# An encoder block on eight cores: a build-time list scheduler for all engines, paired score matmuls, and weights cast through SBUF

## The chip, the cores and the metric

The kernel runs on all eight cores of one Trainium2 chip (two dies of four cores). Each core computes two of the sixteen sequences; the cores exchange nothing. The metric is the device time of the slowest core in microseconds (us), the median of several executions. Such a program has a second, slower state in some of its executions, in which the cores of one die or of both show a lower granted TensorE clock. TensorE is written PE, VectorE DVE, ScalarE ACT, GpSimd POOL; PEld is PE's weight load, which overlaps its matmuls. PV is the matmul of the exponentiated scores with v. Filler is work without a wait of its own (mostly FFN matmuls) that PE runs while an attention step waits. A slab is a block of weights, and a ring is the set of SBUF buffers through which slabs pass.

## The reference, cut to what matters

```python
# x: (16, 2048, 1024) float32; 2 sequences a core
h = rms_norm(x, norm1_g)
lru_x, lru_gate, q, k, v = split(h @ w_in)        # 1024 -> 2560, five slabs of 512 columns
# head group A: causal conv (width 4), RG-LRU (exp, log, scan over positions), times GeLU(lru_gate)
out_a = gelu(lru_gate) * rg_lru(causal_dwconv(lru_x))
# head group B: differential attention, 4 heads, two softmax maps a head (c = 0, 1) over 64 channels each
logits = q_c k_c^T / 8 + bias[rel_bucket(k_pos - q_pos)]          # block-causal in chunks of 64
out_b = rms_norm((softmax_1 - lam * softmax_2) @ v, per head)
x = x + concat(out_a, out_b) @ w_out
# gated FFN, width 3072, causal conv (width 3) on the gate branch
h = rms_norm(x, norm2_g)
gate, val = split(h @ ffn_w_up)                   # 1024 -> 2 x 3072
x = x + (gelu(causal_dwconv(gate)) * val) @ ffn_w_down
out = rms_norm(x, final_norm_g)
```

A core works through eight groups of 512 tokens (four to a sequence). Group g of a sequence attends to the keys of groups 0 to g, so attention grows from group to group and starts small again with the second sequence. The FFN of a group depends only on that group's own mix, apart from two columns of conv history. So the FFN of group g-1 (only matmuls, conv and GELU) can run beside the attention and LRU of group g (short steps with long waits).

## The kernel before

It is written straight through, and an instruction's place on its engine is the place of its call. A helper derives the semaphore waits from the buffers read and written:

```python
def op(self, eng, fn, reads=(), writes=()):
    waits = self._deps(eng, reads, writes)
    self.ecount[eng] += 1
    tok = (("e", eng), self.ecount[eng])
    self.prog[eng].append((fn, waits, tok[0], 1))      # order of calls = order of execution
    self._update(reads, writes, tok)
```

The overlap is made by hand: a window takes the list of attention and LRU steps of group g and the list of FFN units of group g-1, and puts a number of FFN units after each step by a table of weights.

```python
def weight(n):                              # how many FFN units a step deserves
    kind, h, key, _ = users[n]
    if kind == "lru":
        return 1.5
    if kind == "norm":
        return 3.0
    ...
for cur in range(nU):                       # run_window (cut)
    issue(cur + dpt, cur - 1)               # scores one step ahead
    ...
    target = int(math.ceil(cumw[cur + 1] / cumw[nfu] * nF - 1e-9))
    batch = fu[fi:target]                   # FFN units placed here
    ...
    users[cur][1](slot(cur))                # exp and PV of this step
```

Attention handles one softmax map c at a time. Score tiles rotate over two PSUM banks. A tile near the diagonal gets its bias on DVE into SBUF and then a second exp:

```python
op("pe", lambda e: e.matmul(banks[bk][:, 0:N], lhsT=KT[c * 64:(c + 1) * 64, h, j * 128:(j + 1) * 128],
                            rhs=qT[c * 64:(c + 1) * 64, h, q0:G], start=True, stop=True), ...)
if wn:
    op("dve", lambda e: e.tensor_tensor(out=sbn[:, p, 0:wn], in0=banks[bk][:, 0:wn], in1=bias_ap, op=ALU.add), ...)
...
if wn:
    op("act", lambda e: e.activation(out=PT[:, p, 0:wn], in_=sbn[:, p3, 0:wn], func=AF.Exp), ...)
if N > wn:
    op("act", lambda e: e.activation(out=PT[:, p, wn:N], in_=banks[bk][:, wn:N], func=AF.Exp, bias=...), ...)
```

The FFN beside attention owns three PSUM banks, and the down projection of four token tiles therefore goes in passes of at most three accumulators, reading its weights twice:

```python
na = len(acc_banks)                         # 3 beside attention
passes = [list(range(NT))[i:i + na] for i in range(0, NT, na)]
for c2 in range(2):
    for ts in passes:
        accs = acc_banks[:len(ts)]
        for ks in range(3):
            units.append((lambda ...: unit_down(c2, ks, ts, accs), nop, False))
```

The weights arrive as float32 and are needed as bf16. Twenty-five copies, issued by POOL, cast them from HBM to HBM at the start. Every use then loads a slab of 1 MB into a ring of three.

```python
def cast_slab(si, parts):
    for pi, (c0, ncol, src) in enumerate(parts):
        S_.dma("pool", wsl_d[si, :, :, c0:c0 + ncol], src.rearrange("(kk p) c -> p kk c", p=128), ...)
def load_slab(si):
    r = ring_i[0]
    ring_i[0] = (r + 1) % NRING
    S_.dma("sp", ring[:, r, :, :], wsl_d[si], reads=b_slabd[si], writes=[b_ring[r]])
```

The softmax here doesn't subtract the row's maximum and nothing guards it: scores larger than these inputs give would overflow.

## Time and profile before

| | before |
|---|---|
| time, median of 3 fast runs | 2580.04 us (2579.63 to 2582.57) |
| profiled core's span | 2570.9 us |
| PE busy | 1996.0 us, 78% |
| DVE, ACT busy | 1240.6, 1144.8 us (48%, 45%) |
| mean granted clock, eight cores | 0.875 to 0.885 |
| bytes moved | 317.49 MB |

Read such a profile from the engine that does the unavoidable work. Here that is PE. A PE busy for 78% at a mean clock of 0.88 loses twice: in the idle time, and in matmuls that run slowly after it. Next comes the question of what ended the idle time (the waits view), and where in the span it lies (a cut into stretches). The lines themselves stand in the prediction below.

### The profile page before, as it was taken

How to read it: one execution, taken by the hardware profiler on the slowest of the kernel's cores; microseconds unless marked ns; L12 is line 12 of the kernel's file. 1: busy time of each engine (PE TensorE's matmuls, PEld its weight loads, DVE VectorE, ACT ScalarE, POOL GpSimd, SP SyncE). 2: the span in 40 equal slices, each digit the busy share in tenths (PEclk: the TensorE clock that was granted, in tenths of full speed). 3: DMA queues.
4: the chain of work that ended last, by engine and by line, in shares of the span. 5: the costliest groups of instructions: out<-in, count | busy, mean ns of one | idle time of the engine just before them, and what ended most of it. 6: DMA issues, size and time to landing. Idle time of an engine off the chain costs nothing.

```text
span 2570.9 us, 32883 instructions; the slowest of 8 cores (2560.0 to 2570.9 us)
## 1 busy us (share of the span) xinstructions
PE 1996.0 (78%) x9920; PEld 892.2 (35%) x9920; DVE 1240.6 (48%) x2666; ACT 1144.8 (45%) x1861; POOL 143.3 (6%) x152
## 2 busy tenths in 40 slices
PE   1637879688896887979787598878779687788787
PEld 1213334333343333434333343334334343333333
DVE  1355562554625535244663465355563454533562
ACT  1244552545535454454442454344553455545240
POOL 1000000000000000000000000000000000000000
PEclk8758999698996978978999699979899798998899
DMA  9999935431244311343225332443214421124233
GB/s 186 174 108 152 177 105 189 152 107 74 82 164 148 115 49 67 112 185 113 99 99 197 117 129 84 163 180 108 73 68 178 164 99 66 65 91 154 104 129 115
DMA packets 70523, 317.49 MB, mean 123 GB/s; under 512 B 5328, under 2 KB 30928, under 8 KB 39248
## 3 DMA queue, kind: packets, MB, share of 16 engines
q1 hardware_dynamic: 44352, 289.18, 31.9%
q0 software_dynamic: 26000, 26.22, 9.7%
q8 instruction: 85, 1.39, 0.2%
q14 instruction: 86, 0.70, 0.1%
HBM read 324.81 MB, written 42.99 MB: 143 GB/s over the span
## 4 chain that ended last, share of the span: by engine, by line
PE 57%; DVE 16%; ACT 11%; issue 8%; DMA 4%; another core or an unknown queue 2%; POOL 1%; DVEq 1%; ACTq 0%; SPq 0%; POOLq 0%
PE pb L497 26%; PE pb L892 13%; PE pb L818 5%; PE pb L707 5%; PE pb L672 5%; ACT PT L698 3%; DVE aT L511 2%; DVE facc L516 2%; PE pb L592 2%; ACT aT L868 2%; DMA ring<-wslab 2%; DMA wslab<-w_in 2%; ACT facc L506 2%; DVE facc L523 1%
## 5 line engine op out<-in xcount | busy, mean ns | idle before, releaser
L497 PE MATMUL pb<-hT,ring 128*128 128x512 bf16 x4096 | 1003.1, 398 | 80.3 <-DMA ring<-wslab 30.0
L497 PEld LDWEIGHTS pb<-hT,ring 128*128 128x128 bf16 x4096 | 392.0, 101 | 596.9 <-issue 215.1
L707 PE MATMUL pb<-Va,PT 128*128 128x129 bf16 x2176 | 257.0, 243 | 301.4 <-ACT PT L698 254.8
L698 ACT ACTIVATE PT<-pb,prm 128x512 bf16<-128x512 f32 (+3 forms) x512 | 302.1, 608 | 229.4 <-PE pb L672 206.8
L892 PE MATMUL pb<-ring,aT 128*128 128x512 bf16 x1536 | 348.4, 382 | 12.2 <-DMA ring<-wslab 5.5
L707 PEld LDWEIGHTS pb<-Va,PT 128*128 128x128 bf16 x2176 | 161.2, 105 | 471.1 <-issue 424.5
L506 ACT ACTIVATE facc<-pb,prm 128x512 f32<-128x512 f32 x192 | 149.1, 776 | 258.1 <-PE pb L497 175.7
L672 PE MATMUL pb<-qT,KT 64*128 64x512 bf16 (+3 forms) x640 | 237.3, 400 | 8.0 <-ACT thi L645 5.1
L685 DVE TENSOR_TENSOR sbn<-pb,prm 128x256 f32<-128x256 f32 (+1 forms) x304 | 110.3, 371 | 274.7 <-PE pb L672 225.3
L694 ACT ACTIVATE PT<-sbn 128x256 bf16<-128x256 f32 (+1 forms) x304 | 112.0, 372 | 293.6 <-DVE sbn L685 272.2
L884 DVE TENSOR_TENSOR aT<-pb,aT 128x512 bf16<-128x512 f32 x192 | 129.5, 689 | 219.4 <-PE pb L497 195.9
L516 DVE SCALAR_TENSOR_TENSOR facc<-pb,prm,facc 128x511 f32<-128x511 f32 x192 | 143.7, 748 | 149.6 <-ACT facc L506 142.8
L892 PEld LDWEIGHTS pb<-ring,aT 128*128 128x128 bf16 x1536 | 145.0, 98 | 189.8 <-issue 26.8
L511 DVE SCALAR_TENSOR_TENSOR aT<-pb,prm,facc 128x510 bf16<-128x510 f32 x192 | 143.7, 748 | 20.0
L818 PE MATMUL pb<-ring,mixT 128*128 128x512 bf16 x512 | 129.8, 421 | 8.0 <-ACT mixT L801 6.5
L516 DVE SCALAR_TENSOR_TENSOR xc<-pb,prm,xc 128x511 f32<-128x511 f32 (+2 forms) x96 | 71.7, 748 | 112.7 <-ACT xc L506 105.8
L902 DVE TENSOR_TENSOR xg<-pb,xg 128x512 f32<-128x512 f32 x64 | 42.8, 687 | 130.3 <-PE pb L892 116.2
L472 PE MATMUL pb<-ident,hb 128*128 128x128 bf16 x512 | 46.6, 270 | 74.5 <-ACT hb L460 36.0
L433 POOL TENSOR_TENSOR sm<-sm 128x4 f32<-128x4 f32 x36 | 36.3, 1008 | 1186.3 <-DVE sm L424 1186.3
L672 PEld LDWEIGHTS pb<-qT,KT 64*128 64x128 bf16 x640 | 57.1, 95 | 128.1 <-issue 94.7
L868 ACT ACTIVATE aT<-aT 128x2048 bf16<-128x2048 bf16 x48 | 88.2, 1899 | 0.2
L523 DVE SCALAR_TENSOR_TENSOR facc<-fhalo,prm,facc 128x1 f32<-128x1 f32 (+1 forms) x288 | 67.7, 235 | 31.9 <-DVE facc L523 1.6
(105 smaller groups left out, 1468.7 us busy)
## 6 DMA issues: line engine op xcount, KB each, us to landing
ring<-wslab SPq DMA_DIRECT2D x242, 1024.0 KB, 4.9
xg<-x SPq DMA_DIRECT2D x32, 512.0 KB, 6.9
out<-xg SPq DMA_DIRECT2D x32, 512.0 KB, 2.8
wslab<-w_up POOLq DMA_DIRECT2D x12, 1024.0 KB, 88.6
wslab<-w_down POOLq DMA_DIRECT2D x6, 1024.0 KB, 108.2
wslab<-w_in POOLq DMA_DIRECT2D x5, 1024.0 KB, 56.6
wslab<-w_out POOLq DMA_DIRECT2D x2, 1024.0 KB, 99.7
prm<-params SPq DMA_DIRECT2D x1, 1098.5 KB, 7.2
```

The source lines that it names most:

```text
L497: last = e.matmul(banks[bi][:], lhsT=ring[:, r, kk, c * 128:(c + 1) * 128], rhs=src[:, kk, :], start=(kk == 0), stop=(kk == 7))
L506: op("act", lambda e: e.activation(out=acc, in_=ps[:], func=AF.Identity, scale=w_ap[:, nh:nh + 1], bias=b_ap), reads=[b_ps[bi], b_prm], wr ...
L511: op("dve", lambda e, sft=sft, j=j: e.scalar_tensor_tensor(out=last_out[:, sft:G], in0=ps[:, 0:G - sft], scalar=w_ap[:, j:j + 1], in1=acc[ ...
L516: op("dve", lambda e, sft=sft, j=j: e.scalar_tensor_tensor(out=acc[:, sft:G], in0=ps[:, 0:G - sft], scalar=w_ap[:, j:j + 1], in1=acc[:, sf ...
L672: op("pe", lambda e: e.matmul(banks[bk][:, 0:N], lhsT=KT[c * 64:(c + 1) * 64, h, j * 128:(j + 1) * 128], rhs=qT[c * 64:(c + 1) * 64, h, q0 ...
L694: op("act", lambda e: e.activation(out=PT[:, p, 0:wn], in_=sbn[:, p3, 0:wn], func=AF.Exp), reads=[b_sbn[p3]], writes=[b_PT[p]])
L698: op("act", lambda e: e.activation(out=PT[:, p, wn:N], in_=banks[bk][:, wn:N], func=AF.Exp, bias=prm[:, fo + h:fo + h + 1]), reads=[b_ps[b ...
L707: last = e.matmul(banks[abk][:, off:off + 129], lhsT=PT[:, p, (il - i0) * 128:(il - i0 + 1) * 128], rhs=Va[:, j, h, 0:129], start=(j == 0 ...
L818: last = e.matmul(banks[bk][:], lhsT=mixT[:, kk, t * 128:(t + 1) * 128], rhs=ring[:, r, kk, :], start=(kk == 0), stop=(kk == 7))
L868: op("act", lambda e, k4=k4: e.activation(out=aT[:, 4 * k4:4 * k4 + 4, :], in_=aT[:, 4 * k4:4 * k4 + 4, :], func=AF.Gelu_apprx_tanh), read ...
L884: op("dve", lambda e: e.tensor_tensor(out=aT[:, fc, :], in0=banks[bV][:], in1=aT[:, fc, :], op=ALU.mult), reads=[b_ps[bV], b_aT[fc]], writ ...
L892: last = e.matmul(banks[bk][:], lhsT=aT[:, ks * 8 + kk, t * 128:(t + 1) * 128], rhs=ring[:, r, kk, :], start=(ks == 0 and kk == 0), stop=( ...
```

## The change

Its intent is to leave the order to a program. Every call now makes a node with an estimated duration, its reads and writes, a priority and the engines that may run it. A list scheduler simulates the engines at build time, always places the node that can start first (on a tie the one of higher priority), gives out PSUM banks and ring slots as it goes, and only then emits the instructions. Attention steps of group g+1 have higher priority than the FFN of group g, which fills what is left. At the same time: the two maps of a score are computed by two matmuls on different halves of the array into two neighbouring banks, with one bias add in PSUM and one exp over both; the 25 slabs become 50 halves of 0.5 MB, loaded as float32 on first use, cast by ACT or DVE and written back for later uses; conv history moves to POOL in one go.

```diff
+    def schedule(self, policy):
+        ...
+        while placed < len(nodes):
+            best = None
+            for e in engs:
+                for n in avail[e]:                       # (condensed)
+                    t = n.ready + slack.get(e, 0.0)
+                    if t < free[e]: t = free[e]
+                    for v in n.opens:                    # PSUM bank or ring slot that this node opens
+                        f = find_slots(v, t, used)
+                        ...                              # no slot: node can't be placed now
+                    if e == "act" and n.tab is not None and n.tab != cur_tab:
+                        tt = t + (6.0 if left.get(cur_visit, 0) else 1.4)
+                    key = (tt, n.pri, n.i)
+        ...
+        for n, t in order:
+            self._emit_node(n)
...
-NRING = 3
+    NRA, NRF, NPT = 4, 5, 4          # ring halves of projections, of the FFN; exp tiles
...
-        def cast_slab(si, parts): ...                    # HBM to HBM
+            if key not in seen:
+                node({"sp": 0.1}, ... dma_start(out=stg_ap[g.s], in_=src), writes=[g], dma=1048576, tag="ldw")
+                node({"dve": ..., "act": ...}, cast, reads=[g, b_stg], writes=[v, fifo], tag="cast")
+                node({"sp": 0.1}, ... dma_start(out=wsl_d[si], in_=ring[:, v.s, :]), reads=[v], tag="wb")
+            else:
+                node({"sp": 0.1}, ... dma_start(out=ring[:, v.s, :], in_=wsl_d[si]), dma=524288, tag="ld")
...
+                    s = VT(P_ps, n=2, cls="qk")          # two neighbouring banks, always 0 and 1
+                    def qk(e, s=s, j=j, N=N, h=h, i0=i0):
+                        for c in range(2):
+                            last = e.matmul(psum[:, s.s + c, 0:N], lhsT=KT[c * 64:(c + 1) * 64, ...],
+                                            rhs=qT[c * 64:(c + 1) * 64, h, i0 * 128:G], start=True, stop=True)
...
+                    op("act", act_us(2 * N, ptr=1), ... e.activation(out=PT[:, pt.s, :, 0:N],
+                        in_=psum[:, s.s:s.s + 2, 0:N], func=AF.Exp, bias=pv("farb", h, h + 1)), ...)
...
+                accs = [VT(P_ps) for t in range(NT)]     # down projection: four accumulators at once
+                for ks in range(3):
+                    sl = [load_slab(("dn", c2 * 3 + ks, hf), P_F, ringF, pr) for hf in range(2)]
+                    for hf, t in [(hf, t) for hf in range(2) for t in range(NT)]:
+                        op("pe", MMC / 2, f, reads=[sl[hf][0]] + b_aT[...], writes=[accs[t]], tag="dn")
...
+        for gi in range(ngrp):
+            mix, ffn = (gi + 1) * 1000, (gi + 1) * 1000 + 500
+            stage_at(stage_A, mix, gi + 1)               # norm, q, k, v
+            units, convs = stage_at(stage_F1, ffn, gi)
+            stage_at(stage_G, ffn + 1, gi + 1, [units[21]], gi)
+            stage_at(stage_F2, ffn + 2, gi, convs, gi)
+            stage_at(stage_L, mix + 8, gi + 1)           # LRU
+            stage_at(stage_B, mix + 10, gi + 1)          # attention
+            stage_at(stage_C, mix + 20, gi + 1)          # output projection, norm 2
+            stage_at(stage_E, ffn + 5, gi)
+        def slots(v, p):
+            if v.cls == "qk": return (0,)
+            if v.cls == "acc": return (2, 3, 4)          # PV accumulators
+            if attn[1] == 0 and attn[2] == 0:            # no attention step open
+                return (5, 6, 7, 4, 3, 2, 1, 0)
+            return (5, 6, 7)
```

(In the diff many lines are cut, and the loop of the scheduler is condensed.)

## The prediction

> **What bounds the kernel now.** I read the cores view first (eight spans from 2560.0 to 2570.9 us, dies equal, no core at a capped clock), then the page. Its busy list and its slices in tenths say that no engine is full:
>
> ```profile
> PE 1996.0 (78%) x9920; PEld 892.2 (35%) x9920; DVE 1240.6 (48%) x2666; ACT 1144.8 (45%) x1861; POOL 143.3 (6%) x152
> ...
> PEclk8758999698996978978999699979899798998899
> DMA  9999935431244311343225332443214421124233
> ```
>
> PE is busy 78% and the clock dips: 575 us of the span hold no matmul, and part of the 1996 runs slow. DMA is full only in the first five slices (325 us). To see where the idle lies I cut the span at the V projections (end of a group's input stage) and at the first output-projection matmul, which gives "overlap windows" (attention and LRU of group g with the FFN of g-1) and "transitions" (output projection, norms, input projection). Columns: stretch, length, busy of PE, PEld, DVE, ACT, POOL with counts, clock, DMA share, GB/s.
>
> ```profile
> 0.00:109.00 109.00, 46.41 (x192) 20.48 (x192) 20.92 (x47) 21.15 (x34) 12.52 (x21) 0.83 0.99 178
> 109.00:202.00 93.00, 28.91 (x137) 11.89 (x136) 53.41 (x108) 45.17 (x101) 7.52 (x9) 0.52 1.05 125
> ...
> 863.00:1157.50 294.50, 235.72 (x1194) 103.13 (x1193) 128.02 (x285) 148.28 (x241) 16.39 (x16) 0.85 0.28 102
> 1157.50:1221.00 63.50, 58.03 (x290) 28.02 (x290) 27.88 (x52) 25.89 (x41) 0.61 (x1) 0.90 0.31 111
> 1221.00:1441.00 220.00, 156.57 (x712) 66.25 (x711) 123.83 (x277) 84.34 (x137) 17.33 (x16) 0.88 0.39 139
> ```
>
> Group 0 takes 202 us with 75 us of matmul, at half clock in its second part. In the later windows DVE and ACT are busy 38 to 56%, PE 71 to 80%, at clock 0.85 to 0.88. So the bound is latency in a hand-made order: PE meets a step whose input is not there yet and holds up FFN matmuls that could run. The waits view names it:
>
> ```profile
> PE pb L707 <- ACT PT L698: 254.8, 170, 12.8
> PE pb L794 <- DVE ob L743: 61.3, 8, 10.3
> PE pb L707 <- ACT PT L694: 44.1, 34, 4.1
> PE pb L472 <- ACT hb L460: 36.0, 2, 29.2
> ```
>
> (us in total, times, longest.) The PV matmuls wait 299 us for exp, and the transposes wait 61 us at each group's end for the head norm.
>
> **What the Trainium skill says.**
> - "TensorE: Matmul & The Clock Gate", Part 1, The HAM clock gate: PE idle for a window of about 3.4 us falls to half clock and returns when busy. The trace agrees: 0.52 in 109 to 202 us, 1.00 in 1040 to 1105 us where PE is busy 95%. Filling gaps therefore pays twice.
> - The same Part 1 also warns of a limit of 13/16 of the clock once three cores of a die run dense matmuls. The trace differs: from 2515 to 2540 us all eight cores run 115 to 118 matmuls in 25 us (about 0.215 us each), and every one shows 1.00.
> - The same page, Part 3, row tiling: matmuls with a short contraction on different row groups run at once. The timeline agrees: two score matmuls together take what one takes.
>
> ```profile
> 1042.58 0.39 PE L672 MATMUL pb<-qT,KT 64*128 64x512 bf16 x2
> ...
> 1050.37 0.39 PE L672 MATMUL pb<-qT,KT 64*128 64x512 bf16 x1
> ```
>
> - "DMA: Bandwidth & Descriptors", Specifications: about 358 GB/s from HBM per core. The trace: 289.18 MB of the hardware queue in 31.9% of 2570.9 us are 353 GB/s while active.
>
> **The change part by part.**
> 1. *PE work.* The instruction orders of the two programs have the same matmuls (6464 of 512 columns, 640 scores, 2176 PV, 640 transposes). In issue slots at full clock: 6464 x 0.216 (the timeline has 8 in 1.73 us) = 1396; PV 2176 x 0.08 (4 in 0.32) = 174; transposes 640 x 0.09 (46.6 us / 512) = 58. Score slots: before, only 50 of the 320 pairs stand side by side, so 590 slots; after, all 320 do. At about 0.3 us a slot (0.32 for 512 columns, less for short ones) 177 becomes 96. The floor is 1805 us before and 1724 after. Pairing itself saves 81 us of PE.
> 2. *exp and tables.* Rows for 512, 384, 256 and 128 columns (683, 580, 473, 367 ns) give 262 + 0.82 per column, so one exp over 1024 costs 1.10 us. After: 224 x 1.10 + 32 x (0.89 + 0.68 + 0.47) = 312 us, against 302.1 + 112.0 before. One LRU activation less per block saves 32 x 0.63 = 20. Table loads fall from 49 x 1.283 us to about 20, saving 37. Added are 37 weight casts of about 1.9 us (the row of 2048 columns, L868), 70 us. ACT goes from 1145 to about 1056 us. DVE stays near 1230: halo steps -68, casts and LRU steps about +60. Neither was the bound; over 1890 us they are 56% and 65%.
> 3. *Order.* FFN steps are now halves of 4 matmuls (0.86 us), placed between score and PV by estimated times, over any group boundary; the FFN of g starts while the norms of g are still running, so the transitions lose their idle ends. By group: 808 x 0.216 + 80 x 0.09 = 181.7 us without attention (124.4 of it FFN), plus attention of 11.2, 26.2, 41.3, 56.3 us for g = 0 to 3 of a sequence (PV x 0.08 plus pairs x 0.3).
> 4. *Weights.* The 25 casting copies through HBM, issued one per 8 to 16 us until 217 us, go. Instead 50 halves of 1 MB come into two staging buffers, are cast by ACT or DVE, and are written back. For group 0, 14 halves at about 5.5 us (estimate: 1.05 MB at 250 GB/s is 4.2, plus cast and waits) after 13 us of x and parameters make 90 us; attention overlaps, the last projection ends near 115 instead of 218 us. The 36 FFN halves fall into the first overlap window: 36 x 1.57 MB (read and write-back) + about 10 MB of other loads = 67 MB, which at 285 GB/s (below the 353, for 1 to 2 KB rows) is 235 us against 208 us of PE work. That window is DMA-bound.
> 5. *Sum.* 115 (group 0) + 235 + six windows of PE work, 6 x 181.7 + 41.3 + 56.3 + 11.2 + 26.2 + 41.3 + 56.3 = 1323, times 1.06 for stalls that the order cannot foresee (a choice: dense stretches now run at 1.00 to 1.03 of the floor, mixed ones far worse) = 1402 + last FFN and final norm 139 = 1891 us; about 1895 as timed.
>
> **The rivals.**
> - *Imperfect order.* An engine executes the fixed order; where real latencies differ from the estimate, PE waits for exp as now. Scores have one pair of PSUM banks, so a step of score, bias, exp is a serial chain of about 0.32 + 0.1 + 1.1 + 0.3 = 1.8 us; 64 of them are 117 us within a 238 us window. For it: the 299 us of such waits now. Against: a score then has an FFN half to fill its wait. At 1.15 instead of 1.06 the time is 2010.
> - *First use bound by DMA.* If 1 KB rows give only 170 GB/s, the first window takes 390 us instead of 235 and the time is 2050. For it: the casting copies hold the DMA at 0.97 to 1.06 for 325 us today. Against: those move DRAM to DRAM with a cast.
> - *Clock cap.* If unbroken matmuls on all cores trip the 13/16 limit, 1724/0.8125 = 2122 replaces 1724: about 2300. Against: the eight cores at 1.00 above.
> - *PSUM bound.* With attention alive, only three banks serve projections; a gate unit holds one for about 1.73 + 0.78 + 2 x 0.75 + waits = 4.6 us, so one unit per 1.5 us, just under PE's 1.73. It holds, narrowly; a 20% longer hold costs perhaps 60 us.
>
> **Range and chances.** All rivals but the cap leave a gain above 20%, and even the cap leaves 10%. Better than predicted means stalls of 1.02 and a first window at the PE floor: about 1805. Worse means one of the first two rivals in full: about 2030. To come within 2%, several rivals must meet; I give that 3%, slower 1%, faster 96%.
>
> **What would show it.** In the changed profile: PE busy about 90% or more in the middle slices, clock 0.97 to 1.00; the waits of PV for exp below 100 us; 320 score pairs in half the slots; exp over 1024 near 1.10 us; DMA high only until about 350 us; group 0's output projection over by about 115 us; ACT near 1056, DVE near 1230. It would be wrong if the clock reads 0.81 on a die, if the middle windows stay under 85% PE, or if the first window runs past 300 us.

## The result, and the profile after

The changed kernel takes **2089.38 us** (median of four fast runs, 2082.57 to 2095.6) against 2580.14 us for the kernel before in the same rounds. The ratio is 0.809, 95% interval 0.8055 to 0.8121. Ratios in this document are the mean time of one kernel's fast runs over that of the other's of the same rounds, so not quite the ratio of the medians quoted. The direction was right. The time lies outside the range of about 1805 to 2030: the gain is 491 us where 685 were expected.

The same parts of the page as before, busy time and slices in tenths, of the changed kernel:

```profile
PE 1804.5 (86%) x9920; PEld 845.4 (40%) x9920; DVE 1087.7 (52%) x2137; ACT 1070.6 (51%) x1350; POOL 170.1 (8%) x251
...
PEclk9859899999999999879989998999999999977999
DMA  9874478953224623026324541345331462302534
```

PE's busy time fell by 191.5 us and its idle time from 574.9 to 289.6 us. A slice is 52 us long. After the start the clock column is lowest at two places, 840 to 940 us (8, 7) and 1830 to 1940 us (7, 7). DMA is high until about 420 us, with a lull (4) from 157 to 262 us.

To hold the result against the prediction's sum I cut the span at the last down-projection matmul of each group (the first cut is the end of group 0's output projection). Columns: stretch, length, busy of PE, PEld, DVE, ACT, POOL with counts, clock, DMA share, GB/s.

```profile
0.00:167.00 167.00, 85.47 (x440) 39.86 (x440) 79.23 (x150) 98.36 (x128) 20.91 (x36) 0.80 0.79 231
167.00:424.80 257.80, 217.68 (x1145) 98.78 (x1144) 140.00 (x270) 143.56 (x157) 16.95 (x26) 0.94 0.70 218
...
679.40:961.70 282.30, 252.19 (x1481) 122.80 (x1480) 134.64 (x263) 152.53 (x190) 20.54 (x28) 0.90 0.32 109
961.70:1183.40 221.70, 198.68 (x1001) 91.73 (x1000) 128.20 (x258) 100.07 (x143) 19.81 (x30) 0.95 0.39 134
...
1670.80:1951.50 280.70, 250.63 (x1481) 121.90 (x1480) 134.39 (x263) 152.41 (x190) 20.44 (x27) 0.91 0.30 103
1951.50:2094.00 142.50, 126.35 (x576) 54.94 (x574) 69.71 (x144) 37.41 (x45) 6.22 (x8) 0.97 0.43 149
```

| term of the sum | predicted, us | measured, us | difference |
|---|---|---|---|
| group 0 to its output projection | 115 | 167 | +52 |
| first window | 235 | 258 | +23 |
| six windows | 1323 x 1.06 = 1402 | 1526.7 = 1323 x 1.154 | +125 |
| last FFN and final norm | 139 | 142.5 | +3 |

The windows are the stretches between two cuts; the floor is the prediction's sum of PE's issue slots at full clock. The largest miss is the factor on the six windows. Their PE is idle for 151.5 us, and its busy time is 52 us above the floor. I read these 52 us as the lowered clock (0.90 to 0.96 in these windows); with experiment 1's clock of 0.96 to 0.99 the same windows have 1332 us of busy PE, 9 above the floor.

The groups that concern attention (columns: line, engine, operation, shapes, count, busy time and mean ns of one, then idle time before them and what ended most of it):

```profile
L959 ACT ACTIVATE PT<-pb,prm 128x1024 bf16<-128x1024 f32 (+1 forms) x320 | 314.9, 984 | 248.4 <-PE pb L941 96.6
...
L941 PE MATMUL pb<-qT,KT 64*128 64x512 bf16 (+3 forms) x640 | 125.6, 384 | 97.9 <-ACT PT L959 97.4
L968 PE MATMUL pb<-Va,PT 128*128 128x129 bf16 x2176 | 201.2, 239 | 4.7 <-ACT PT L959 3.0
```

PV (L968) waits 3.0 us for exp where it waited 299 before. The wait has partly moved to the next score (L941), which waits 97.4 us until exp has emptied the one pair of score banks. That is a third of the old wait. The timeline of PE shows a part of it in a long attention, where PE has no FFN matmul left to put in between (start, duration; x is the number of matmuls in a run; brackets hold the idle time before and its releaser):

```profile
862.81 0.39 PE L941 MATMUL pb<-qT,KT 64*128 64x512 bf16 x2
863.13 0.63 PE L968 MATMUL pb<-Va,PT 128*128 128x129 bf16 x8
863.60 1.03 PE L1099 MATMUL pb<-ringF,aT 128*128 128x512 bf16 x4
...
866.42 0.39 PE L941 MATMUL pb<-qT,KT 64*128 64x512 bf16 x2 [0.85 <-ACT PT L959]
866.74 0.63 PE L968 MATMUL pb<-Va,PT 128*128 128x129 bf16 x8
868.22 0.39 PE L941 MATMUL pb<-qT,KT 64*128 64x512 bf16 x2 [0.85 <-ACT PT L959]
...
915.20 9.63 PE L1099 MATMUL pb<-ringF,aT 128*128 128x512 bf16 x36
```

Until 864.6 us every score and PV is followed by four matmuls of the down projection (L1099). Then they are gone for 50 us. At 915.2 us, when the last PV of the attention is done, they come back in one run of 36. A step now takes 1.8 us (866.42 to 868.22): this is the serial chain of score, exp and PV that the prediction's first rival had described, and the filler that was to hide it is missing. The same stretch in columns as above, and two others that matter later:

```profile
840.00:865.00 25.00, 25.00 (x173) 11.95 (x172) 8.83 (x16) 12.47 (x13) 1.02 (x1) 1.00 0.11 38
865.00:915.00 50.00, 31.74 (x220) 18.86 (x220) 11.70 (x21) 23.80 (x25) 1.01 (x1) 0.56 0.00 1
125.00:150.00 25.00, 2.61 (x8) 0.69 (x8) 14.21 (x26) 15.18 (x22) 7.33 (x10) 0.50 0.81 225
1040.00:1050.00 10.00, 4.85 (x29) 2.76 (x30) 9.55 (x22) 6.49 (x11) 0.61 (x1) 0.58 0.00 0
```

With filler PE is busy 25.00 of 25 us at clock 1.00. Without it 31.7 of 50 at 0.56. These 31.7 us hold some 22 steps; at the 0.95 us that score and PV take at 866.42 us, they would be 21 us (an estimate). In the third line PE has next to nothing to do at the end of group 0. In the fourth DVE is busy for 9.55 of 10 us.

**Why the filler ends: a lock-out** (read from the code and the trace). While attention runs, the scheduler gives other work three banks, 5, 6 and 7. The down projection opens four accumulators of one bank each. Three can be opened, and the fourth tile of each weight half has to wait for a bank until attention is over. The weight halves that this tile still needs stay in the FFN ring, and the ring has five. So three tiles x five halves x four matmuls = 60 matmuls can run, and the trace has 60 of them between 841.5 and 864.6 us. After that nothing of the FFN can go on. This lies in the two groups with the longest attention (the windows of 282 and 281 us); the second one has its 60 matmuls between 1831 and 1854 us and then the same 50 us without filler.

### The profile page after: what moved, and what is told of

The parts are those of the page before. It is cut to its first block, busy times and chain, and to the rows that moved or that the text cites. A ratio compares the mean times of both kernels' runs of the same rounds, so it can differ in the third digit from the quotient of the medians.

```text
span 2094.1 us, 30805 instructions; the slowest of 8 cores (2073.4 to 2094.1 us)
## 1 busy us (share of the span) xinstructions
PE 1804.5 (86%) x9920; PEld 845.4 (40%) x9920; DVE 1087.7 (52%) x2137; ACT 1070.6 (51%) x1350; POOL 170.1 (8%) x251
## 4 chain that ended last, share of the span: by engine, by line
PE 60%; ACT 11%; issue 10%; DMA 9%; DVE 8%; POOL 1%; SPq 0%; DVEq 0%; ACTq 0%; POOLq 0%
PE pb L774 28%; PE pb L1099 13%; PE pb L792 7%; PE pb L968 5%; PE pb L941 4%; ACT PT L959 4%; DMA ringA<-wslab 3%; ACT facc L1058 2%; DMA ringF<-wslab 2%; DMA Va<-w_down 2%; PE pb L745 1%; DVE aT L1064 1%; ACT aT L1078 1%; DMA KT<-w_in 1%; DMA Va<-w_up 1%
## 5 line engine op out<-in xcount | busy, mean ns | idle before, releaser
L774 PE MATMUL pb<-hT,ringF 128*128 128x512 bf16 x3072 | 734.6, 389 | 44.5 <-DVE aT L1069 12.5
L774 PEld LDWEIGHTS pb<-hT,ringF 128*128 128x128 bf16 x3072 | 290.2, 100 | 409.9 <-issue 115.7
L959 ACT ACTIVATE PT<-pb,prm 128x1024 bf16<-128x1024 f32 (+1 forms) x320 | 314.9, 984 | 248.4 <-PE pb L941 96.6
L1099 PE MATMUL pb<-ringF,aT 128*128 128x512 bf16 x1536 | 355.3, 386 | 13.1 <-ACT ringF L705 10.7
L774 PE MATMUL pb<-hT,ringA 128*128 128x512 bf16 x1024 | 242.8, 387 | 24.2 <-ACT ringA L705 6.2
L1099 PEld LDWEIGHTS pb<-ringF,aT 128*128 128x128 bf16 x1536 | 147.8, 99 | 194.6 <-issue 37.9
L941 PE MATMUL pb<-qT,KT 64*128 64x512 bf16 (+3 forms) x640 | 125.6, 384 | 97.9 <-ACT PT L959 97.4
L968 PE MATMUL pb<-Va,PT 128*128 128x129 bf16 x2176 | 201.2, 239 | 4.7 <-ACT PT L959 3.0
L968 PEld LDWEIGHTS pb<-Va,PT 128*128 128x128 bf16 x2176 | 153.6, 106 | 86.2 <-issue 53.8
L758 POOL TENSOR_TENSOR sm<-sm 128x1 f32<-128x1 f32 (+1 forms) x128 | 94.2, 743 | 1140.5 <-DVE sm L755 1053.9
L774 PEld LDWEIGHTS pb<-hT,ringA 128*128 128x128 bf16 x1024 | 98.0, 99 | 146.3 <-issue 43.8
L792 PE MATMUL pb<-ringA,mixT 128*128 128x512 bf16 x512 | 116.5, 383 | 11.2 <-POOL mixT L913 11.2
L941 PEld LDWEIGHTS pb<-qT,KT 64*128 64x128 bf16 x640 | 35.2, 94 | 179.6 <-issue 167.2
```

The lines of the kernel that those rows point to most:

```text
L758: op("pool", 1.0, lambda e: e.tensor_tensor(out=smv(rsn, 0, n), in0=smv(ssn, 0, n), in1=smv("mhalf").to_broadcast([128, n]), op=ALU.pow), ...
L774: last = e.matmul(bank(p), lhsT=w[:, kk, cc * 128:(cc + 1) * 128], rhs=src[:, kk, :], start=(kk == 0), stop=(kk == 7))
L792: last = e.matmul(bank(p), lhsT=src[:, hf * 4 + kk, t * 128:(t + 1) * 128], rhs=w[:, kk, :], start=(hf == 0 and kk == 0), stop=(hf == 1 an ...
L941: last = e.matmul(psum[:, s.s + c, 0:N], lhsT=KT[c * 64:(c + 1) * 64, j // NT, h, (j % NT) * 128:(j % NT + 1) * 128], rhs=qT[c * 64:(c + 1 ...
L959: op("act", act_us(2 * N, ptr=1), lambda e, s=s, pt=pt, N=N, h=h: e.activation(out=PT[:, pt.s, :, 0:N], in_=psum[:, s.s:s.s + 2, 0:N], fun ...
L968: last = e.matmul(psum[:, acc[ab].s, off:off + 129], lhsT=PT[:, pt.s, c, (il - i0) * 128:(il - i0 + 1) * 128], rhs=Va[:, j, h, 0:129], sta ...
```

## The experiments

The windows are numbered 1 (ending at 424.8 us in the changed kernel) to 8. Every edit is against the changed kernel. The list scheduler plans the whole program anew after each edit, so an edit moves more than it names; differences below about 20 us are hard to put down to one cause.

**Theories.** L (lock-out): banks and ring shut out the down projection in long attention. D (bunching): where attention, LRU and gate conv coincide, DVE is locally full. P (pairing): 81 us of PE work are the pairing's. Q: the single pair of score banks costs as much in waits as the pairing saves. W: weights on first use come late, at the start. The rival of L and D together is that the order itself is worth what it is and that the remaining idle time is scattered latency.

### 1. Other ring sizes (theory L)

```diff
-    NRA, NRF, NPT = 4, 5, 4
+    NRA, NRF, NPT = 2, 7, 4
```

> Only the split of nine weight buffers changes: FFN 7 and mixing 2 instead of 5 and 4. Theory A (lock-out): with attention alive, three PSUM banks serve the down projection, so its fourth token tile cannot open; with five buffers all of them hold weights that the fourth tile still needs, and after 60 matmuls the FFN stands still (841 to 915 us and 1831 to 1905 us). Seven buffers hold the six halves of a column half, so three tiles can finish and the fourth follow. It expects the down projection to run on beside attention in those two windows, their length down by about 30 to 45 us each, some gain in the others, and about 2000 us (1980 to 2020). Rival B (the chain score, bias, exp is the path, and filler would not shorten it): the windows keep their 282 and 281 us, the time 2070 to 2110.

Measured: correct, 1979.99, 1982.95 and 1979.93 us (one slow run of 2186.2 left out), ratio 0.7685 [0.7667, 0.7702]. That is 109 us below the changed kernel for the same SBUF. The timeline of PE in the same attention, a cut around it, and windows 3 and 7:

```profile
836.16 0.39 PE L941 MATMUL pb<-qT,KT 64*128 64x512 bf16 x2
836.48 2.76 PE L1099 MATMUL pb<-ringF,aT 128*128 128x512 bf16 x12
839.08 0.62 PE L968 MATMUL pb<-Va,PT 128*128 128x129 bf16 x8
839.63 0.39 PE L941 MATMUL pb<-qT,KT 64*128 64x512 bf16 x2
```

```profile
821.00:887.00 66.00, 64.72 (x454) 32.23 (x452) 21.19 (x36) 32.18 (x37) 3.53 (x4) 1.00 0.23 72
...
657.30:886.10 228.80, 220.34 (x1378) 106.14 (x1376) 120.65 (x240) 143.89 (x181) 18.78 (x26) 0.99 0.37 118
...
1553.00:1837.80 284.80, 259.54 (x1582) 124.97 (x1582) 150.05 (x289) 154.14 (x192) 21.79 (x29) 0.96 0.36 118
```

Now the down projection runs through the attention; all 192 of its matmuls for this group lie inside, in place of 60. PE is busy 64.7 of 66 us at clock 1.00. The waits of scores for exp fall from 97.4 to 40.1 us in all, PE's idle time from 289.6 to 221.4 us, and its busy time from 1804.5 to 1757.0 us, at a higher clock (0.956 to 0.962 on the cores, from 0.928 to 0.933). The six windows sum to 1427 us, a factor of 1.079 over the 1323 us floor. **The lock-out is gone in both windows**: both attentions have filler until they end. But the gain does not lie where theory A had put it, 30 to 45 us in each of windows 3 and 7. Window 3 is 53 us shorter, and window 4 gives 14 of them back. Window 7 is not shorter at all (284.8 against 280.7 us): there the new plan fills the attention with up-projection matmuls (485 with those of the input projection, in place of 328), has 65 of the down projection inside, and the time was saved before it, 33 us in window 6 and 23 in window 5. The rest is 15 us in window 1 and 8 in window 2. So this run alone does not separate the lock-out from a deeper FFN ring, which gives PE more to choose from everywhere.

### 2. Two accumulators at a time, ring as it was (theory L, by another way)

```diff
-                accs = [VT(P_ps) for t in range(NT)]
+                for ts in (((0, 1), (2, 3)) if c2 == 0 and ngrp > gi + 1 and (gi + 1) % 4 == 3
+                           else ((0, 1, 2, 3),)):
+                    accs = {t: VT(P_ps) for t in ts}
```

(The loads and matmuls move into the loop, so the six weight halves are read twice there.)

> Buffers as in the changed kernel, but in the two windows beside the longest attention the first column half of the down projection runs as two passes of two token tiles, which three banks can hold; its 3 MB of weights are loaded twice there. Theory A: the lock-out goes without any more buffers, these two windows lose 20 to 40 us each, the others stay, about 2030 us (2010 to 2050). Rival B, or a rival C (deeper prefetch is what helped the first run): no change there, 2070 to 2110.

Measured: correct, 2061.56, 2066.48, 2071.49 us, ratio 0.8017 [0.7986, 0.8048]. The two windows with the locked attention are 250.5 and 251.9 us where they were 282.3 and 280.7, so 32 and 29 us shorter, as expected, with no more buffers: the matmuls of the down projection inside the long attention go from 60 to 149 and 148 (some records are missing in this trace). But the time fell by only 23 us, and misses the expected 2010 to 2050. The next window is 240.4 (221.7 before) and the last part 155.7 (131.4): I read this as the work that ran early being missing as filler later, above all at the last group's second norm; no run tests that. So the lock-out's cost is shown in its own two windows, 61 us of the 125, and lifting it saved the whole program only about a third of that.

### 3. One map at a time (theories P and Q)

```diff
-                    s = VT(P_ps, n=2, cls="qk")
+                    for c in range(2):
+                        s = VT(P_ps, cls="qk")
+                        ...                      # score, bias, exp and PV for map c alone
...
-                return (0,)
+                return (0, 1)
```

> Undoes the pairing alone: two score matmuls, two exps over at most 512 columns and two PV parts per key block, each score in its own bank of the same two. Theory P (the prediction's part 2): up to 81 us more PE slots and about 100 us more ACT time come back, part of it hidden: 2140 to 2190 us. Rival Q: two banks that free one by one let the next score start before the whole exp is done, which takes PE's 97 us of waits for exp down and pays for the lost pairing: 2075 to 2115 us.

Measured: correct, 2173.9 to 2176.93 us, ratio 0.8458 [0.8439, 0.8477], so 87 us slower than the changed kernel. The group rows:

```profile
L957 ACT ACTIVATE PT<-pb,prm 128x512 bf16<-128x512 f32 (+3 forms) x640 | 384.1, 623 | 170.5 <-PE pb L947 74.8
L947 PE MATMUL pb<-qT,KT 64*128 64x512 bf16 (+3 forms) x640 | 234.8, 416 | 59.0 <-ACT PT L957 56.1
```

The scores take 234.8 us of PE instead of 125.6. Their waits for exp do fall, from 97.4 to 56.1 us, as Q says, but they do not pay for it. In this plan the pairing is worth 87 us, and I had put it at 81. That the two agree is partly luck: PE's busy time grows by 147 us (109 in the scores, 69 in PV, other groups less), its idle time falls by 66, and the edit splits exp and PV as well, so that the score slots alone are not measured.

### 4. Casting through HBM again (two tries)

```diff
-            if key not in seen:
-                ...                              # load float32, cast, write back
-            else:
-                node({"sp": 0.1}, ...)
+            node({"sp": 0.1}, lambda e: e.dma_start(out=ring[:, v.s, :], in_=wsl_d[si]), ...)
+        for k_, key in enumerate(first):         # 50 casting copies, HBM to HBM
+            node({"pool": 0.85}, lambda e, ...: e.dma_start(out=wsl_d[si]..., in_=w_src(key)), ...)
```

> Undoes the weights' path alone: all fifty halves are cast by copies through HBM issued at the start, in the order of first use; loads are bf16 from the first group on; no cast on ACT or DVE. Theory R: the copies hold the DMA for about 300 us as in the kernel before, the first output projection comes at 190 to 230 us instead of 167 and the first FFN ends at 450 to 500 us instead of 425; the rest is unchanged: 2130 to 2180 us. Rival S (the first two windows are bound by LRU and PE anyway): 2075 to 2105 us.

Measured: correct, 2266.97 to 2288.43 us, ratio 0.8849, 182 us slower than the changed kernel and above what any theory had said. The trace shows that the test was unfair: the 50 issues hold POOL's queue, and the first norm's power step on POOL came so late that PE had its first matmul only at 174 us. So a second try lets at most four copies be in flight, starts them after the parameters have landed, and takes the small POOL steps of the first groups to ACT and DVE:

```diff
+            node({"pool": 0.85}, ..., reads=[b_prm] + b_stage if k_ < 4 else [],
+                 writes=[b_slabd[si], b_win[k_ % 4]], ...)
...
+            if early[0]:
+                ...                              # rstd as exp(-0.5 ln) on ACT; other POOL steps on DVE
```

> The weights' path undone again, mended: at most four casting copies in flight, the first after parameters and x have landed, and the norms' power and the small POOL steps of the first two groups moved to ACT and DVE, so that the copies hold up no computation in POOL's queue. Theory R: the copies still take about 5.5 us a half, the FFN weights come no sooner than at 280 us, the first FFN ends at 440 to 480 us instead of 425: 2105 to 2150 us. Rival X: the 182 us of the first try came from the copies' flood and from POOL's queue alone, and the cast through SBUF is worth nothing by itself: 2070 to 2105 us.

Measured: correct, 2214.86, 2216.58, 2218.64 us, ratio 0.8593 [0.8577, 0.8608]. Still 127 us slower than the changed kernel, and above the 2105 to 2150 that I had expected. The cut up to the end of group 0's output projection and of the first window:

```profile
0.00:284.30 284.30, 98.31 (x417) 42.02 (x424) 75.90 (x150) 77.58 (x138) 38.15 (x54) 0.72 1.02 139
284.30:537.70 253.40, 216.53 (x1141) 101.36 (x1162) 136.11 (x274) 111.71 (x165) 3.84 (x11) 0.95 0.44 120
```

All of it is in group 0: 284 us against 167. The windows that follow are as long as in the changed kernel (253.4 against 257.8, and the six within 6 us of theirs). In those 284 us DMA is full (1.02). The 139 GB/s beside it must not be held against the changed kernel's 231: a copy is counted here with the 0.5 MB of bf16 that it writes and not with the 1 MB of float32 that it reads, where the changed kernel's loads count the float32. The 50 copies (26.2 MB as written) run from 28 to 316 us, and 43 of them are done by 284 us, FFN weights mostly, where the changed kernel has loaded 21 halves by 167 us; a load of 0.5 MB among the copies takes 11 us at the median, against 3.8 for the projection ring's loads in the changed kernel.

This second try is not fair either. PE waits 107.6 us for slabs of the projection ring, 92 of them in group 0, and the longest wait is this one (PE's timeline, the DMA issues on SP, the queue of SyncE, and SP's waits up to 285 us):

```profile
129.58 4.15 PE L795 MATMUL pb<-ringA,hT 128*128 128x512 bf16 x12 [39.49 <-DMA ringA<-wslab]
...
70.29 0.32 SPq L695 DMA_DIRECT2D ringA<-wslab  x1
117.11 0.32 SPq L695 DMA_DIRECT2D ringF<-wslab  x1
117.62 0.46 SPq L695 DMA_DIRECT2D ringA<-wslab  x1
...
SPq L367 <- DMA wslab<-w_up: 49.3, 2, 46.4
```

The copies of all ten halves of the input projection had landed by 91 us. But in SP's order an FFN slab's load (ringF) stood first, and SP waited 46 us for the copy of that slab; the load that PE needed was issued only after it. So of the 117 us of group 0 about 40 belong to the order of this plan's issues. That the cast through SBUF is worth 127 us is not shown; shown is that loads beside the casting copies take three times as long, and that both tries with copies lost time in group 0 alone.

### 5. The order itself

```diff
+                    if n.i != placed:            # place nodes in the order of creation
+                        continue
...
-            if attn[1] == 0 and attn[2] == 0:
+            if True:                             # all PSUM banks for all work
```

> The same operations, pairing and weights' path, but placed in the order in which the program creates them, with no list scheduling. Theory V: the order is what makes the gain: each key block costs about 2.3 us on PE's clock (score 0.32, bias 0.7 in some, exp 1.1, PV 0.6), 320 of them 740 us, LRU blocks 32 x 12 = 384, FFN 8 x 130, projections 8 x 60 and 50 first loads exposed, in sum above 2800 us. Rival W: pairing and the weights' path carry most of the gain and it stays below the 2580 us of the kernel before.

Measured: correct, one look, 3908.33 us, PE 55% busy, mean clock 0.71, and 576.0 us of waits of PV for exp, 320 times. All parts of the change but the order are in it. So the scheduler is not a refinement here: in the order of creation, which puts whole stages one after another, the other parts of the change do not even reach the kernel before. What they are worth in the hand-made order of that kernel was not tested.

### 6. The LRU later (theory D)

```diff
-                stage_at(stage_L, mix + 8, gi + 1)
+                stage_at(stage_L, mix + 12, gi + 1)
```

> Only the priority of the LRU stage changes: behind two heads of attention instead of ahead of all. Theory D (bunching): in every window attention, LRU and the gate branch's convolution fall on the same 40 us, DVE is 85 to 100% busy there and PE half idle at half clock; the LRU later meets the value branch, which needs less of DVE. It expects 5 to 10 us less in each of six windows, about 2045 us (2025 to 2065). Rival E (PE waits there for PSUM banks and latency, whatever the order): 2075 to 2105.

Measured: correct, 2058.2 to 2060.06 us in four fast runs, ratio 0.7988 [0.7972, 0.8003], 30 us below the changed kernel. Windows 3 and 7 are 13 and 8 us shorter and the others 0 to 5 us, where 5 to 10 us had been expected in each of six. That a single number of the priority table gives 1.4% says that the plan is not at its best, but not yet why.

### 7. Less work for DVE (theory D), wrong on purpose

```diff
-                op("dve", ..., thi = thi * xc)                     # one LRU multiply
-                D_(dve_us(512), ... O1 = O1 * rs)                  # three steps of the head norm
-                D_(dve_us(512), ... O2 = O2 * rs2n)
-                D_(dve_us(512), ... O1 = O1 + O2)
```

> Wrong result on purpose: three of the head norm's steps and one LRU multiply are dropped, 4 x 0.69 us x 32 = 88 us of DVE work that reads and writes SBUF alone and holds no PSUM bank. Theory D (DVE is locally full): the bunched stretches shorten by a good part of their share, 4 to 8 us a window, about 2045 us (2025 to 2065). Rival E (banks): 2075 to 2100.

Measured: 2026.82 to 2042.01 us, ratio 0.7894 [0.7846, 0.7941], 55 us below the changed kernel. Its output is wrong, which doesn't matter for the time. DVE's busy time falls by 79 us to 1008.9 us (50% of the span). So work on an engine that is half idle over the span can still cost time. The gain is not even over the windows, as expected (4 to 8 us each), but lies in windows 1, 4 and 5 (19, 14 and 13 us). This agrees with the stretch at 1040 us in window 4 shown above, where DVE is busy 9.55 of 10 us and PE 4.85. But the next run limits what may be concluded.

### 8. Both at once: is D a limit of its own?

The ring sizes of experiment 1 with the cuts of experiment 7 (wrong), and with the later LRU of experiment 6:

> Both at once: buffers 7 and 2, and the dropped 88 us of DVE steps (wrong result on purpose). If lock-out (A) and the locally full DVE (D) are separate causes, their gains of 108 and 55 us add up: about 1926 us (1910 to 1945). If they are one cause, the stretch that the FFN leaves open being the one in which DVE is behind, the second gain is mostly gone: 1960 to 1985 us.

> Rings of 2 and 7 halves (alone 1981) together with the LRU's later priority (alone 2059, 30 below the changed kernel). If the two lift separate limits the gains add: 1945 to 1955. If both only give PE something to do during the same stretches of attention, the second gains nothing once the first is there, as it went with the shortened head norm: 1970 to 1990.

Measured: the first gives 1989.15, 1989.57 and 2013.49 us in fast runs, ratio 0.7743 [0.7686, 0.7799]. The second is correct and gives 1999.43, 2001.03 and 2016.56 us in fast runs, ratio 0.7751 [0.7666, 0.7836]. Ring sizes alone gave 0.7685. Neither adds anything; both medians are a little slower, and slower than the 1960 to 1985 and 1970 to 1990 us expected of one common cause. So with the ring opened, the two edits are worth nothing, although they had been worth 55 and 30 us before. **That D is a limit of its own is not shown.**

Why they don't add is not shown either. Against the ring sizes alone, the cut makes windows 3 and 7 shorter by 19 and 16 us and windows 1, 4 and 8 longer by 12, 29 and 16; with the later LRU window 7 is 45 us shorter and window 8 is 38 us longer. What is won in one window is given back in another, as in experiment 2, and a new plan can do that by itself. The slices of 10 us in which DVE is over 90% busy hold 47 us of PE's idle time in the changed kernel and still 34 us with the ring opened, so the traces don't say that full stretches of DVE have become free.

### 9. Group 0 (theory W)

The order of group 0 with its LRU first (gate and LRU slabs and steps ahead of q, k, v), alone and with the ring sizes of experiment 1:

```diff
-        stage_at(stage_A, 0, 0)
-        stage_at(stage_G, 5, 0, (), "g")
-        stage_at(stage_L, 8, 0)
+        stage_at(stage_A, 0, 0, 0)               # norm only
+        stage_at(stage_G, 1, 0, (), "g")
+        stage_at(stage_L, 2, 0)
+        stage_at(stage_A, 3, 0, 1)               # then q, k, v
```

> In group 0 alone gate and LRU weights are loaded first and the LRU starts ahead of attention. Theory T: the first output projection waited for four LRU blocks of about 12 us each whose weights came last, at 92 us; it ends at 140 to 150 us instead of 167, and the whole program is 10 to 25 us shorter: 2065 to 2080 us. Rival U: the next window is bound by the first loads of the FFN weights, so that the gain is given back there: 2080 to 2100 us.

> Candidate for the fastest correct version: buffers 7 and 2, and group 0's gate and LRU ahead of its attention. Theory T: the 13 us that the LRU's order saved in group 0 stay to the end here: about 1968 us (1960 to 1975). Rival U (given back to the first loads or lost in the new plan): 1975 to 1990 us.

Measured: alone one fast run of 2083.95 us (three others slow), which says little beside the changed kernel's 2082.57 to 2095.6; the trace has group 0's end at 153.5 instead of 167.0 us and window 1's at 405 instead of 424.8, of which 7 us are given back in window 7. With the ring sizes there are two fast runs, 1974.66 and 1977.33 us, against 1979.93 to 1982.95 without it; correct. It is the fastest correct version by about 5 us, too little for so few runs to be called shown.

Half of the bytes on first use (wrong): each half slab is read only to the half, and cast twice from it, so that casts, write-backs and matmuls stay.

```diff
-                    out=stg_ap[g.s].rearrange("p (kk c) -> p kk c", kk=kkn), in_=src), ... dma=1048576
+                    out=stg_ap[g.s][:, 0:1024].rearrange("p (kk c) -> p kk c", kk=kkn // 2),
+                    in_=src[:, 0:kkn // 2]), ... dma=524288
```

> Wrong on purpose: on first use each half of a weight slab is loaded only to the half (0.5 MB instead of 1 MB) and the cast reads that half twice, so casts, write-backs and matmuls stay what they are and only the HBM read of first use is halved. Theory W (group 0's 52 us and the first window's 23 us over my prediction are weights arriving late): group 0's output projection ends at 115 to 135 us instead of 167, the first window takes 215 to 240 us instead of 258, the whole gains 50 to 90 us, about 2000 to 2040. Rival S (group 0 is a chain of serial LRU and attention steps at half clock that starts when the x tiles are there, whatever the weights): group 0 ends at 150 to 167, the first window within 10 us of 258, the whole 2065 to 2090.

Measured: 2067.47 to 2068.55 us in three fast runs, ratio 0.798 [0.7921, 0.8038]. Group 0 ends at 152.8 us and window 1 takes 238.6 us where it took 257.8. So theory W has window 1 right, where half of the bytes are worth 19 us; in group 0 they are only 14 of the 52, as its rival S had said, and the whole time is S's too. For the rest, group 0 without the LRU's gates and scan (wrong), alone and with half of the bytes:

```diff
+                if gi == 0:
+                    ...                          # mixT = gg * xc in place of the LRU; the conv stays
+                    continue
```

> Wrong on purpose: in group 0 alone the LRU's gates, exponentials and scan are left out (its convolution and the multiply with the gate stay), so that group 0 has no serial LRU chain; everything else is as in the changed kernel. Halving the bytes moved the end of group 0's output projection from 167 only to 153 us, so some 38 us of the 52 are still to be named. If the serial LRU (four blocks of about 12 us after the last weights) is the rest: 167 falls to 120 to 135 us. If the attention and the head norms of group 0 at half clock set the end as well: 145 to 160 us.

> Wrong on purpose: half the bytes of first use and no LRU chain in group 0, together. If late weights and the LRU chain are all of the 52 us, group 0's output projection ends near 110 to 120 us, which is what I had predicted for the whole. If a third cause holds it (attention steps at half clock, 93 to 140 us in the halved kernel), 125 to 145 us.

Measured: 144.8 us and 150.0 us for the end of group 0 (2077.23 and 2054.23 us in all). Both speak for a third cause. But the two edits together end later than the second alone, and above the 125 to 145 us expected; why is open, and with one look each differences of a few us mean little. The end of group 0 on PE in the changed kernel, then without the LRU:

```profile
136.52 0.59 PE L1006 MATMUL pb<-ident,ob 128*128 128x128 bf16 x4 [9.16 <-DVE ob L998]
...
150.05 11.64 PE L792 MATMUL pb<-ringA,mixT 128*128 128x512 bf16 x44 [11.17 <-POOL mixT L913]
```

```profile
126.99 0.59 PE L1013 MATMUL pb<-ident,ob 128*128 128x128 bf16 x4 [8.56 <-DVE ob L1005]
128.31 11.11 PE L792 MATMUL pb<-ringA,mixT 128*128 128x512 bf16 x44 [0.74 <-DVE mixT L1022]
```

In the changed kernel the output projection (L792) waits 11.17 us for the last block of the LRU. Without the LRU the projection starts 22 us earlier, and then stands behind the last head norm, for which the transpose (L1013) waited 8.56 us. So at least two chains end within some 20 us of each other: the LRU, whose four blocks follow its projection (done at 95 us) with scans at 106, 125, 136 and 147 us, and attention with its head norms, both at half clock (0.50 between 100 and 150 us) and with no FFN of an earlier group beside them. Taking one away uncovers the next, and even without late weights and LRU the end is 30 us or more above my 115. That attention at half clock is what then sets the end is read from the trace and not tested.

## Why the prediction was wrong, step by step

**What failed.** The step is in part 5 of the change: "times 1.06 for stalls that the order cannot foresee (a choice: dense stretches now run at 1.00 to 1.03 of the floor, mixed ones far worse)". Measured it is **1.154**, 125 us on the six windows. The form of the step (PE work with a factor for an imperfect order) was right; what was mis-sized is the factor, and behind it one omission. The rival "imperfect order" had named 1.15 and 2010 us. Its number was luck: it expected the chain of score, exp and PV to show all along, because estimates and real times differ, and set against it that "a score then has an FFN half to fill its wait". It is this filler that failed. My rival on PSUM looked at the gate units, which hold one bank for a few microseconds each. It did not look at the down projection, which needs four banks at once where attention leaves three. The kernel before had the passes of three accumulators for that reason, and the change dropped them, which the diff shows. The trace and experiments 1 and 2 show the lock-out. Experiment 2, which lifts it by another way, takes 61 of the 125 us out of the two windows; how much of it a program keeps depends on the later windows. With the ring opened the six windows are 100 us shorter and the factor is 1.079, of which the deeper ring may have a part. What makes up the rest of the 125 us is not shown.

**Group 0, 115 against 167 us.** I took the arrival of the slabs for its end ("14 halves at about 5.5 us ... make 90 us; attention overlaps"). The arrival was nearly right (the ten halves of the input projection have landed by 79 us, the four of the output projection by 106 us). What failed is "attention overlaps": a chain of four LRU blocks and the rest of attention still follow, at half clock and with nothing beside them. Experiment 9 has 14 us for the weights and 22 us for the LRU (not additive), and leaves some 30 us that are not tested apart.

**First window, 235 against 258 us.** I called it DMA-bound at 285 GB/s. The trace has 218 GB/s at a DMA share of 0.70, so the DMA engines were not full. With the FFN ring of seven the same window moves 274 GB/s and takes 243 us; halving the bytes brings 238.6 us; and in the first try of experiment 4, which had all casts done before, it takes 224.2 us. So late weights cost up to some 34 us here. That the ring held the loads back, and not the DMA engines, is how I read the first two of these numbers. The rival "390 us" is refuted.

**What held.** Pairing: 81 us predicted, 87 when undone (by more PE work and less idle time, see experiment 3). The exp over both maps: 1.10 us a piece predicted, 1.112 us in the group by shape. ACT: 1056 us predicted, 1070.6 measured. Table loads: about 20 predicted, 18 in the trace. Waits of PV for exp: "below 100", 3.0 measured, with the new wait of the scores at 97.4. DMA is high until about 420 us, in place of 350. The clock limit did not appear in fast runs.

**What else was off.** The transposes' 61 us of waits for the head norm are the sum of eight waits, and not 61 us at each group's end. DVE: "stays near 1230", it fell to 1087.7 us. In the groups, the conv-history steps fell from 116.6 to 33.6 us, as planned, but work that either engine may do also went to ACT: copies of q, k, v and the PV sums from 81.8 to 25.8 us, squares and scalings of the norms from 61.8 to 25.4 us. The clock: 0.97 to 1.00 in the middle predicted, 0.90 to 0.96 in the six windows; the lowest stretches are those of the lock-out (0.56), and of group 0 (0.50). And I had summed DVE and ACT over the whole span ("over 1890 us they are 56% and 65%"), where stretches with DVE at 95% were to come. Whether these bind by themselves stays open (experiment 8).

**Not settled.** How the 116 us by which experiment 1's trace is shorter divide between the lock-out and a deeper ring; why gains do not add in experiment 8; what the cast through SBUF is worth against copies whose loads do not block each other; what of group 0's last 30 us is attention at half clock; and whether the LRU's place in experiment 6 acts through DVE or through the filler that it leaves.

## What to carry to other kernels

An order that never leaves an engine idle while a step is ready is only as good as its filler: list, for the stretch that has the most waits, which buffers and banks the filler needs at once, and compare it with what that stretch leaves free; four accumulators against three free banks shut out a third of the FFN for 50 us in each of two windows, and ring sizes that cost no memory gave 109 us. Test causes together as well as alone, because two edits that each save 30 to 100 us may add nothing. Look at every window and not only at the one that an edit aims at, since a gain there can be given back later. And when a prologue seems bound by its loads, look for the serial chains that end just behind them, since halving the bytes moved group 0 by 14 of 52 us only.

## What the Trainium skill lacked or had wrong

- "TensorE: Matmul & The Clock Gate", Part 1, says that three cores of a die with dense matmuls take the die to 13/16 of the clock within about 5 to 20 us, and that one should plan with that. In the fast executions here it doesn't: with experiment 1's kernel, in the stretch of 66 us shown, the eight cores' PE is busy for 54.9 to 64.7 us at clocks of 0.93 to 1.00, and their means over the span are 0.956 to 0.962. Lowered dies appear in single executions only: in a slow run of the half-bytes kernel one die reads 0.828 to 0.833 and the other 0.886 to 0.899, at 2228 us against 2068.
- "DMA: Bandwidth & Descriptors", in the table of what SWDGE and HWDGE can do, says that a cast during DMA has to be issued by GpSimd, but gives no rate for a casting copy from HBM to HBM. The run (experiment 4, second try): 50 copies, 26.2 MB as written and twice that as read, from 28 to 316 us, in which they fill 90% of the DMA engines' time; loads of 0.5 MB beside them take 11 us, against 3.8 us for the projection ring's in the changed kernel.
- No page that I found treats the case that an accumulation over many weight loads opens more PSUM banks than are free beside another stage, and then keeps its ring slots as well. The run: 60 matmuls, then 50 us of PE at 31.7 us busy and a clock of 0.56.
